# Low part of the third and fourth rows of the first weights, placed ahead of the third rows of Zl in VectorE's order

## The chip, the core and the metric

The kernel runs on one core of a Trainium2 chip. The core has a matrix engine (TensorE, called PE in the profile, with its weight loads as PEld), a vector engine (VectorE, DVE), a scalar engine (ScalarE, ACT), GpSimd (POOL) and a sync engine (SP) that issues most DMAs. Each engine runs its own instructions in the order in which they stand in its program, and waits on semaphores for the others. The metric is the device time of one execution in microseconds (us). A name with "q" behind it (SPq, DVEq) is the engine's sequencer, which issues and waits.

## The reference

One decoder block for x of 512 tokens by 1024 channels: an RMS norm, one wide input projection, two attention branches with 8 heads of 64 each (forgetting attention "f" and block-sparse attention "m"), gates, two projections back, a merge, an output projection and a residual add.

```python
h = rms_norm(x, norm_g[layer])
proj = h @ w_in[layer]
fq, fk, fv, fz, mq, mk, mv, mz, ga, gb, fl = split_cols(proj, IN_SPLITS)
q = rms_norm(to_heads(fq, FOX_HEADS), fox_q_g[layer])
k = rms_norm(to_heads(fk, FOX_HEADS), fox_k_g[layer])
...
merged = (jax.nn.sigmoid(ga + b_gate[layer, 0]) * (y_fox @ w_fox[layer])
          + jax.nn.sigmoid(gb + b_gate[layer, 1]) * (y_moba @ w_moba[layer]))
x = x + merged @ w_out[layer]
```

The change touches only the start: the product of x, scaled by the norm's gain, with the first 256 columns of w_in ("fqa", the queries of the first four forgetting heads).

## The kernel before, in words

**Products in two parts.** Every matrix operand is split into a high part h (rounded by a copy into the type fp32r) and a low part l, which is the operand less its high part. A product is the sum of three: high by high, high by low and low by high. So each operand costs a copy, mostly on ScalarE, and a subtraction on VectorE.

**Rows.** The 1024 channels are eight groups of 128, called rows 0 to 7 here; "the third rows" is row 2 and "the third and fourth rows" are rows 2 and 3. For row k, `XT[k]` is that part of x transposed (128 channels by 512 tokens), loaded as tile xt. `split_x` makes from it Zh (line 130, ScalarE: x times the gain) and Zl (line 132, VectorE). The weights of fqa come in two halves of four rows, loaded as wr_fqa; `first_split` makes wh_fqa (lines 163 or 165) and wl_fqa (line 167). In the first half it takes row 0, row 1 and then rows 2 and 3 together; in the second half rows 4 and 5, then 6 and 7. Its argument `between` says which rows of x are split behind each of these steps.

**First products.** `first_qk` (lines 390 to 392) goes over the eight rows and in each over four groups of 128 tokens: wh by Zh (line 390), wl by Zh (391), wh by Zl (392), 12 matmuls of 256 columns a row. The same function does fka (264 columns) from the same Z. TensorE's order among these three lines within a row is chosen by the planner described below.

**What follows.** The statistics of x give a factor r for each token, which norm_row (line 248) spreads by a transpose into a row rbc (line 249, ScalarE). `normalise` then makes the normalised operand Gh and Gl (lines 253 to 255). The gate products fza and fzb (lines 413 to 415) still use Z; fva (lines 314 to 316) is the first to use Gh and Gl. xf (line 323) is the input of the forget gates, lines 336 to 344 normalise queries and keys (the last steps on GpSimd), line 352 makes the low part of the values fva and so frees their bank of PSUM. Lines 459 to 497 compute the forget gates on VectorE. The attention, the gates and the output projection follow; the last result is added at line 977 and stored at 979.

**The order.** The program is laid out by a planner that simulates the engines' times and lets each engine take what it expects to be ready first. Where the text says `with behind():`, the instruction is tied behind the one that was last put on VectorE, so that the planner cannot take it out of turn. In the first products every cast and subtraction on VectorE is tied in this way, so VectorE's order there is the order of the text: a chain.

The call (line 1048) and the order that results on VectorE before the change: Zl of row 0, the weights of row 1, Zl of row 1, Zl of row 2, wl of rows 2 and 3, Zl of row 3.

```python
first_split(0, ((0,), (1, 2), (3,)))
first_split(1, ((4, 5), (6, 7)))
```

Of the kernel before, what the change touches and what calls it, by code (L numbers as in the profile page):

```python
# [29 lines left out]
def fox_moba_kernel(ctx: ExitStack, tc, xT, x, w_in, w_fl, w_fox, w_moba, w_out, cst, rope, out):  # L30
# [85 lines left out]
    def behind(engine=mybir.EngineType.DVE):  # L116
        return tc.issue_after(last_on(engine))
# [6 lines left out]
    def split_x(*ks):  # L124
        for k in ks:
            Z[k] = [stage["pool"].tile([P, S], F32R, name=f"Z{hl}{k}") for hl in "hl"]
            for c in (slice(0, 256), slice(256, S)) if k == 0 else (slice(0, S),):
                xt = XT[k][:, c]
                zh, zl = (z[:, c] for z in Z[k])
                A.activation(zh, xt, AF.Copy, scale=col(C_NG + k))  # L130
                with behind():
                    V.scalar_tensor_tensor(zl, xt, col(C_NG + k), zh.bitcast(F32), op0=OP.mult, op1=OP.subtract)
# [21 lines left out]
    def first_split(hf, between):  # L154
        raw = RAW[hf]
        hi = sb.tile([P, 4, 264], F32R, name=f"wh_fqa{hf}", tag="wh", bufs=4)
        lo = sb.tile([P, 4, 264], F32R, name=f"wl_fqa{hf}", tag="wl", bufs=4)
        for q, xs in enumerate(between):
            k = slice(2 * q, 2 * q + 2) if hf else slice(max(q, 2 * q - 2), max(q + 1, 2 * q))

            if hf == 0 and q < 2:
                with behind():
                    V.tensor_copy(hi[:, k, :CW], raw[:, k])
            else:
                A.activation(hi[:, k, :CW], raw[:, k], AF.Copy)
            with behind():
                V.tensor_tensor(out=lo[:, k, :CW], in0=raw[:, k], in1=hi[:, k, :CW].bitcast(F32), op=OP.subtract)
            split_x(*xs)
        chunks.setdefault("fqa", []).append((hi, lo))
# [875 lines left out]
        for u in filler(names):  # L1045
            u()

    first_split(0, ((0,), (1, 2), (3,)))
    first_split(1, ((4, 5), (6, 7)))
    nc.sync.dma_start(out=wfl, in_=w_fl)  # L1050
    load_fl("fka", COLS["fka"], 0)
# [184 lines left out]
```

## Time and profile before

| what | us |
|---|---|
| median of three runs | 425.41 (425.33 to 425.57) |
| the profiled execution | 425.42 |
| its span | 423.7 |
| TensorE busy | 417.6 |
| VectorE busy | 327.4 |
| ScalarE busy | 279.6 |
| GpSimd busy | 101.8 |

The profile is of one execution. A row of the timeline gives the start in us from the span's start, the duration, the engine, the line of the kernel, the operation, the tile written and the tiles read, the shapes and how many instructions are merged in the row; a bracket gives the idle time of the engine ahead of it and who ended it. Matmuls overlap: one of 256 columns shows 0.28 us, though the next starts about 0.12 us behind it. The ends of matmuls are modelled, their starts are measured. A row of the view of waits has the waiting engine, tile and line, whom it waited for, the total in us, how often, and the longest.

### The profile page before, as it was taken

The numbers are of one execution on the slowest core, as the hardware profiler recorded it, in microseconds if no ns is written. First come the engines' busy times: TensorE is split into PE (matmuls) and PEld (weight loads), VectorE is DVE, ScalarE is ACT, GpSimd is POOL, SyncE is SP. The second block draws the span as 40 slices with busy tenths as digits, with TensorE's granted clock in tenths as the row PEclk, the third lists the DMA queues.
The fourth block names the chain that finished last, engine by engine and source line by source line (L and its number), as shares of the span: only waits on it lengthen the run. The fifth ranks groups of instructions, "written<-read, shape, count | busy, mean of one in ns | idle before, by whom it ended". The sixth has DMA issues, their size and how long they took to land.

```text
span 423.7 us, 7681 instructions
## 1 busy us (share of the span) xinstructions
PE 417.6 (99%) x2912; PEld 388.2 (92%) x2912; DVE 327.4 (77%) x575; ACT 279.6 (66%) x528; POOL 101.8 (24%) x120
## 2 busy tenths in 40 slices
PE   7999999999999999999999999999999999999996
PEld 6998899999999998899998888899999989988885
DVE  3669978799968778668666779767979698689883
ACT  5877327877877869569757687656656535686450
POOL 1055620223235550015660100340000000022230
PEclk9999999999999999999999999999999999999999
DMA  7972334576253123213032310673141603697484
GB/s 238 389 282 97 95 105 140 154 214 195 79 179 102 28 100 101 84 42 99 28 99 68 108 50 27 227 259 109 27 176 63 236 2 105 216 252 123 99 138 161
DMA packets 24484, 56.10 MB, mean 132 GB/s; under 512 B 2824, under 2 KB 7616, under 8 KB 24448
## 3 DMA queue, kind: packets, MB, share of 16 engines
q1 hardware_dynamic: 13536, 38.11, 27.3%
q0 software_dynamic: 3392, 8.39, 8.7%
q10 hardware_dynamic: 7520, 9.11, 6.6%
q8 instruction: 23, 0.38, 0.4%
q14 instruction: 13, 0.11, 0.1%
HBM read 48.11 MB, written 6.32 MB: 128 GB/s over the span
## 4 chain that ended last, share of the span: by engine, by line
PE 97%; DMA 1%; SPq 0%; DVE 0%; issue 0%; ACT 0%; DVEq 0%
PE pb_GB L769 3%; PE pb_GA L769 3%; PE pb_GA L766 3%; PE pb_GB L766 3%; PE pb_GB L768 3%; PE pb_GA L768 3%; PE po L957 3%; PE po L956 3%; PE po L955 3%; PE pv L627 2%; PE lg L572 2%; PE pv L626 2%; PE lg L571 2%; PE pf L696 2%; PE pf L695 2%; PE pf L697 2%
## 5 line engine op out<-in xcount | busy, mean ns | idle before, releaser
L342 POOL TENSOR_TENSOR ff<-ss,mh 128x8 f32<-128x8 f32 x16 | 29.5, 1845 | 73.7 <-DVE ss L340 52.1
L576 ACT ACTIVATE p<-p,negm 128x128 f32<-128x128 f32 (+1 forms) x64 | 35.8, 560 | 13.3 <-DVE negm L574 12.3
L574 DVE CUSTOM_DVE_ANT_0 p<-lg,mask 128x128 f32<-128x128 f32 (+1 forms) x64 | 30.8, 486 | 14.9 <-PE lg L572 14.6
L904 POOL DMA_DIRECT2D wr_o<-in_w_out_dram x4 | 4.9, 1224 | 95.6 <-ACT wr_o L903 91.9
L142 DVE TENSOR_TENSOR wl_GA<-wr_ga,wh_GA 128x1024 fp32r<-128x1024 f32 x14 | 16.9, 1223 | 5.8 <-ACT wh_GA L140 3.8
L140 ACT ACTIVATE wh_GA<-wr_ga 128x1024 fp32r<-128x1024 f32 x14 | 14.6, 1060 | 10.0 <-PE pb_GA L768 5.1
L140 ACT ACTIVATE wh_GB<-wr_gb 128x1024 fp32r<-128x1024 f32 x14 | 14.6, 1060 | 9.5 <-PE pm L696 3.5
L571 PE MATMUL lg<-KH,QS 128*128 128x128 f32 (+1 forms) x64 | 20.4, 328 | 0.0
L918 DVE TENSOR_TENSOR wl_o<-wr_o,wh_o 128x1024 fp32r<-128x1024 f32 x14 | 17.0, 1222 | 3.8 <-ACT wh_o L917 3.8
L917 ACT ACTIVATE wh_o<-wr_o 128x1024 fp32r<-128x1024 f32 x14 | 14.8, 1061 | 7.2 <-PE pb_GB L768 2.8
L142 DVE TENSOR_TENSOR wl_GB<-wr_gb,wh_GB 128x1024 fp32r<-128x1024 f32 x14 | 16.9, 1222 | 3.5 <-ACT wh_GB L140 3.5
L652 DVE TENSOR_TENSOR ypair<-pv,ysh 64x512 f32<-64x512 f32 x16 | 11.0, 687 | 6.6 <-ACT ysh L651 6.3
L546 DVE SCALAR_TENSOR_TENSOR KL<-p_kT,cs,KH 64x512 fp32r<-64x512 f32 x16 | 12.0, 748 | 3.4 <-ACT KH L543 3.3
L651 ACT ACTIVATE ysh<-pv 64x512 f32<-64x512 f32 x16 | 9.5, 595 | 7.4 <-PE pv L627 4.2
L623 DVE TENSOR_TENSOR ptl<-p_a,pth 128x512 fp32r<-128x512 f32 x16 | 11.0, 685 | 4.2 <-ACT pth L622 4.2
L336 DVE TENSOR_REDUCE ss<-sq 128x8 f32<-128x512 f32 x16 | 10.8, 680 | 4.4 <-ACT sq L335 4.3
L766 PE MATMUL pb_GA<-Gh,wh_GA 128*128 128x256 f32 x48 | 13.6, 283 | 0.0
L769 PE MATMUL pb_GA<-Gh,wl_GA 128*128 128x256 f32 x48 | 13.5, 281 | 0.0
L768 PE MATMUL pb_GA<-Gl,wh_GA 128*128 128x256 f32 x48 | 13.5, 281 | 0.0
L769 PE MATMUL pb_GB<-Gh,wl_GB 128*128 128x256 f32 x48 | 13.5, 281 | 0.0
L768 PE MATMUL pb_GB<-Gl,wh_GB 128*128 128x256 f32 x48 | 13.4, 281 | 0.0
L766 PE MATMUL pb_GB<-Gh,wh_GB 128*128 128x256 f32 x48 | 13.3, 281 | 0.0
(461 smaller groups left out, 1794.8 us busy)
## 6 DMA issues: line engine op xcount, KB each, us to landing
wr_ga<-in_w_in_dram SPq DMA_DIRECT2D x8, 512.0 KB
wr_gb<-in_w_in_dram SPq DMA_DIRECT2D x8, 512.0 KB
wr_o<-in_w_out_dram SPq DMA_DIRECT2D x8, 512.0 KB
xt<-in_xT_dram SPq DMA_DIRECT2D x8, 256.0 KB
x<-in_x_dram SPq DMA_DIRECT2D x8, 256.0 KB
s_dramh<-sum_sh ACTq DMA_DIRECT2D x8, 256.0 KB
s_draml<-sum_sl ACTq DMA_DIRECT2D x8, 256.0 KB
wr_wf<-in_w_fox_dram SPq DMA_DIRECT2D x4, 512.0 KB
```

The lines of the kernel that those rows point to most:

```text
L140: A.activation(hi[:, :, 0:n], src, AF.Copy)
L142: eng.tensor_tensor(out=lo[:, q, 0:n], in0=src[:, q], in1=hi[:, q, 0:n].bitcast(F32), op=OP.subtract)
L342: G.tensor_tensor(out=f2, in0=ss.rearrange("p t h -> p (t h)"), in1=mh, op=OP.pow)
L571: T.matmul(lg[:, :n], qs[:, qt], kh[:, :n], start=True, stop=False)
L574: V.tensor_tensor_reduce(pt, lg[:, :n], mask[:, 512 - n:512], -0.125, 3.0e38, op0=OP.add, op1=OP.min, accum_out=mkn[:, hh, i:i + 1])
L576: A.activation(pt, pt, AF.Exp, bias=mkn[:, hh, i:i + 1], scale=-1.0, accum_out=rs[:, hh, i:i + 1])
L766: T.matmul(o, hi[:, k, cc], lh, start=(n < 3 and c == 0 and k == 0), stop=False, skip_group_check=True)
L768: T.matmul(o, hi[:, k, cc], ll, start=False, stop=False, skip_group_check=True)
L769: T.matmul(o, lo[:, k, cc], lh, start=False, stop=(k == 3), skip_group_check=True)
L917: A.activation(wide(hi), wide(R[key, c]), AF.Copy)
L918: V.tensor_tensor(out=wide(lo), in0=wide(R[key, c]), in1=wide(hi).bitcast(F32), op=OP.subtract)
L955: T.matmul(o, gh, hi[:, c, r, :], start=(new and k == 0), stop=False, skip_group_check=True)
```

## The change

In the first half of the weights, row 2 of x is no longer split in the step of row 1 but in the last step, with row 3, behind the weights' rows 2 and 3. On VectorE the subtraction wl_fqa of rows 2 and 3 (line 167) now stands in front of Zl of row 2 (line 132), and Zl of row 3 follows as before. ScalarE's order stays Zh of row 1, wh of rows 2 and 3, Zh of row 2, Zh of row 3. The planner, fed with this, also chooses other orders on TensorE inside the first products, on VectorE, ScalarE and GpSimd around 30 to 50 us, and for two instructions on TensorE near 289 and 300 us.

```diff
-    first_split(0, ((0,), (1, 2), (3,)))
+    first_split(0, ((0,), (1,), (2, 3)))
     first_split(1, ((4, 5), (6, 7)))
```

## The prediction, as put on record before the changed kernel ran

> **What bounds the kernel now.** I read the page first: the span, the busy shares, the granted clock and the shares of the chain that ended last.
>
> ```profile
> span 423.7 us, 7681 instructions
> PE 417.6 (99%) x2912; PEld 388.2 (92%) x2912; DVE 327.4 (77%) x575; ACT 279.6 (66%) x528; POOL 101.8 (24%) x120
> PEclk9999999999999999999999999999999999999999
> PE 97%; DMA 1%; SPq 0%; DVE 0%; issue 0%; ACT 0%; DVEq 0%
> ```
>
> TensorE (PE) is busy for 99% of the span at full clock and makes up 97% of the chain. So a microsecond counts only if TensorE stands still in it. The view of the waits, for TensorE alone, lists every such place.
>
> ```profile
> PE warm_ps L104 <- DVE fg_pre L479: 1.1, 1, 1.1
> PE fqa L391 <- DVE wl_fqa L167: 0.7, 1, 0.7
> PE fqa L390 <- DVE wh_fqa L163: 0.5, 1, 0.5
> PE fqa L390 <- ACT Zh L130: 0.3, 1, 0.3
> ```
>
> There are four, all in the first products. The change aims at the second: line 391 waits for a low part of the first weights. After it TensorE waits for nobody until its last product. The timeline around it, in order of time (start, duration, engine, line):
>
> ```profile
> 7.75 0.75 DVE L132 SCALAR_TENSOR_TENSOR Zl<-xt,cs,Zh 128x512 fp32r<-128x512 f32 x1
> 7.94 0.63 ACT L165 ACTIVATE wh_fqa<-wr_fqa 128x512 fp32r<-128x512 f32 x1 [0.84 <-DMA wr_fqa<-in_w_in_dram]
> 8.78 1.38 ACT L130 ACTIVATE Zh<-xt,cs 128x512 fp32r<-128x512 f32 x2 [0.21 <-DMA xt<-in_xT_dram]
> 9.54 0.75 DVE L132 SCALAR_TENSOR_TENSOR Zl<-xt,cs,Zh 128x512 fp32r<-128x512 f32 x1 [1.05 <-ACT Zh L130]
> 9.56 0.73 PE L390 MATMUL fqa<-wh_fqa,Zh 128*128 128x256 f32 x4 [0.28 <-ACT Zh L130]
> 10.21 0.68 DVE L167 TENSOR_TENSOR wl_fqa<-wr_fqa,wh_fqa 128x512 fp32r<-128x512 f32 x1
> 10.95 0.39 PE L391 MATMUL fqa<-wl_fqa,Zh 128*128 128x256 f32 x1 [0.66 <-DVE wl_fqa L167]
> 12.00 0.28 PE L390 MATMUL fqa<-wh_fqa,Zh 128*128 128x256 f32 x1
> ```
>
> VectorE (DVE) ends the Zl of the second rows at 8.50 and then idles 1.05 us for the third rows' Zh. The inputs of the low part have been there since 8.57 (7.94 + 0.63), but it stands behind that Zl and runs only at 10.21. TensorE, through with its four line-390 products, waits for it until 10.95.
>
> **The change part by part.** Nothing is added or taken away: the same instructions run with the same operands, no DMA changes its place on SP's, ACT's or POOL's queue, and only VectorE's order is meant to change: low part (L167), then the third rows' Zl, then the fourth rows'.
>
> *Low part.* It can start when ScalarE's high part ends, 8.57, plus the handoff seen at the Zl (Zh's first half of the 1.38 us ends at 8.78 + 0.69 = 9.47, the Zl starts at 9.54: 0.07). So it runs 8.64 to 9.32, inside the 1.05 us in which VectorE idles. Price: nothing.
>
> *The Zl behind it.* Its input comes at 9.47 and VectorE is free at 9.32, so it stays at 9.54 and ends at 10.29. The fourth rows' Zl moves up to 10.21 from 10.81.
>
> *TensorE.* Its undisturbed pace is shown by
>
> ```profile
> 13.44 0.64 PE L390 MATMUL fqa<-wh_fqa,Zh 128*128 128x256 f32 x4
> 13.92 0.64 PE L391 MATMUL fqa<-wl_fqa,Zh 128*128 128x256 f32 x4
> ```
>
> four products in 0.48 us, 0.12 each; four in a group show 0.64. The group at 9.56 shows 0.73, so its restart after a wait cost 0.09, which stays. Line 391 could then begin at 9.56 + 0.09 + 0.48 = 10.13 instead of 10.95: **0.82 us**. The eight products from 10.95 to 12.00 took 1.05 where eight at pace take 0.96; that second restart, **0.09 to 0.10**, goes as well. In the changed program four line-391 products stand ahead of four line-392, so the Zl is needed at 10.13 + 0.48 = 10.61 and is there at 10.29, with 0.32 to spare. Sum at the fourth rows: **0.92 us**. The nearest rows bound it: 0.66, what the row at 10.95 itself counts as idle, and 1.0, if the first restart shrinks too. I take 0.92, since starts are measured while ends of products are modelled.
>
> *What is late next.* The fourth rows start at 11.08; their Zh (second half of the 1.38) is there at 10.16. The fifth start at 12.50, and the later rows at 1.42 each, so the first products end near 18.1 and fka begins there. Its second line needs these:
>
> ```profile
> 14.94 1.06 ACT L140 ACTIVATE wh_fka<-wr_fka 128x1024 fp32r<-128x1024 f32 x1 [0.61 <-DMA wr_fka<-in_w_in_dram]
> 16.04 1.23 DVE L142 TENSOR_TENSOR wl_fka<-wr_fka,wh_fka 128x1024 fp32r<-128x1024 f32 x1 [0.52 <-ACT wh_fka L140]
> 19.56 0.29 PE L391 MATMUL fka<-wl_fka,Zh 128*128 128x264 f32 x1
> ```
>
> The low part of fka ends at 17.27 and is now wanted at 19.56 - 0.92 = 18.64: 1.37 us of cover are left, and a wait would begin only when a DMA of these weights came later than that.
>
> *VectorE from 30 to 60 us.* The program is laid out by a planner, and it also reorders here: two small xf (L323) and one reduction (L336) move ahead of the eight normalising instructions (L253).
>
> ```profile
> 30.38 0.23 DVE L323 SCALAR_TENSOR_TENSOR xf<-fka,r,cs 128x8 f32<-128x8 f32 x1 [0.99 <-ACT qn_fka L321]
> 30.56 0.60 ACT L249 ACTIVATE rbc<-p_rbc 128x512 f32<-128x512 f32 x1 [0.29 <-PE p_rbc L248]
> 31.19 3.31 DVE L253 SCALAR_TENSOR_TENSOR xt<-xt,cs,rbc 128x512 f32<-128x512 f32 x4 [0.58 <-ACT rbc L249]
> 39.26 1.27 DVE L336 TENSOR_REDUCE ss<-sq 128x8 f32<-128x512 f32 x2
> 57.54 0.41 DVE L352 TENSOR_TENSOR v_fva<-pj_fva,v_fva 128x256 fp32r<-128x256 f32 x1
> 59.12 0.28 PE L314 MATMUL pj_fva<-wh_fva,Gh 128*128 128x256 f32 x1
> ```
>
> From 31.19 on VectorE has no idle time until 60. The squares for the moved reduction go in front of rbc on ScalarE, which by the rows puts rbc's end near 31.3 and L253 near 31.4, 0.2 later than now; in return 0.6 for the reduction and some 0.14 for each xf leave the stretch. It ends 0.6 to 0.9 earlier, almost in step with TensorE. Who waits for its end is the third fva product, whose bank L352 frees: 57.95 against 59.12, 1.17 us of cover. If the stretch did not move at all, 0.25 would be left. Price: nothing.
>
> *The rest.* Two more swaps on TensorE, near 289 and 300 us (p_rinv behind one product, one L768 behind some others), change its order and not its work. Later order on VectorE, ScalarE and POOL is unchanged, and every transfer there starts when a buffer is freed, so it moves with TensorE. The end moves whole:
>
> ```profile
> 419.90 0.28 PE L957 MATMUL po<-wh_o,mg 128*128 128x256 f32 x1
> 420.22 0.42 DVE L977 TENSOR_TENSOR ot<-po,eo 128x256 f32<-128x256 f32 x1 [0.88 <-PE po L957]
> 420.67 0.36 SPq L979 DMA_DIRECT2D out_dram<-ot  x1
> ```
>
> Sum: the profiled execution took 425.42, its span 423.70 and 1.72 around it; 425.42 - 0.92 = **424.50 us**. The median of the runs shown, 425.41, is the same within 0.01.
>
> **The rivals.**
>
> *Part of the gain only.* The 0.32 us ahead of the Zl is thin. If the low part starts over 0.2 us later than I have it, it pushes the Zl; with 0.66 gained the time is 424.76, and with the bound of half the gain lost 424.96. For it: handoffs of 0.1 to 0.2 us in the rows. Against it: both inputs are early.
>
> *It does not do what it says.* If the low part were held by something other than its place, it would still end near 10.9: 425.42. The 1.05 us of idle time with its inputs ready speak against it.
>
> *VectorE's stretch slips, and the time ends slower.* POOL's multiplications of fka (L344) move with the reduction from 50.64 to two places inside the stretch. The rows show that such a neighbour costs VectorE time:
>
> ```profile
> 50.64 2.38 POOL L344 TENSOR_TENSOR qn_fka<-qn_fka,ff 128x512 f32<-128x512 f32 x2
> 51.01 1.04 DVE L468 TENSOR_SCALAR fg<-fg 128x32 f32<-128x32 f32 x1
> 52.35 1.75 DVE L142 TENSOR_TENSOR wl_fqb<-wr_fqb,wh_fqb 128x1024 fp32r<-128x1024 f32 x1
> 55.51 1.21 DVE L142 TENSOR_TENSOR wl_fqb<-wr_fqb,wh_fqb 128x1024 fp32r<-128x1024 f32 x1
> 57.44 0.17 DVE L474 SCALAR_TENSOR_TENSOR fg<-fg,fg 128x32 f32<-128x32 f32 x1
> ```
>
> Beside it a small operation took 1.04 instead of some 0.17 and a low part 1.75 instead of 1.21: 1.4 us lost already. Two full holds would be 2.38, so the move is worth between 1.4 less and 1.0 more. The Trainium skill, SBUF — State Buffer, section "Who interferes with whom", says that a VectorE instruction with two SBUF inputs and a GpSimd instruction that reads SBUF exclude each other for the whole instruction; the 1.75 agrees. By that rule alone, with both moved multiplications holding a neighbour fully, the time would be at most 424.65. The place is the third fva product: with the 1.0 the stretch ends 0.4 later at worst than now, TensorE waits 0.15, and 424.65 results. A stretch later by 1.17 than now takes the whole gain (425.42), and later by 2.02 makes the kernel slower by 0.85; at 2.5 the time would be 426.75. That needs 1.6 us more than the rows give, so the chance is small, mostly for planner moves that I have not seen through.
>
> **How the numbers follow.** Forecast (424.35 to 424.65): 0.68. Part of the gain: 0.15. Nothing gained: 0.08. Slower: 0.09. A measurement of this kernel tells about 0.2% from no change, 0.85 us, so faster begins below 424.56; the forecast lies only 0.06 under that line, and I put 0.56 of its 0.68 below it, with 0.02 from the others. Faster 0.58, same 0.33, slower 0.09. The range 424.3 to 425.0 takes in the bounds 0.66 and 1.0 and the half gain, and leaves out nothing gained, slower and about 0.02 under it.
>
> **What would show it.** Right: L167 starts at 8.6 on VectorE, the third rows' Zl stays at 9.54, line 391 loses its wait, the fourth rows start near 11.1, fka near 18.1, and the last product starts near 419.0. Wrong: the low part runs after 9.5, a wait of line 392 on Zl, a wait of the third fva product on L352, or a shift at 18 us that is smaller at 420.

## The result, and the profile after

| | before | changed |
|---|---|---|
| median | 425.41 us (16 runs, 424.94 to 425.97) | 424.62 us (16 runs, 424.15 to 424.99) |
| ratio, 95% interval | | 0.9981 (0.9974 to 0.9989) |
| the profiled execution, its span | 425.42, 423.7 | 424.43, 422.5 |

The changed kernel is 0.79 us faster by its medians; the interval goes from 0.47 to 1.11 us. That is 0.19%, just short of the 0.2% that the prediction took as the line between "same" and "faster". A later comparison of the same two kernels, with 29 and 11 runs, gave 0.77 us by the medians (ratio 0.9985, 0.9976 to 0.9993).

The page of the changed kernel, and TensorE's waits:

```profile
span 422.5 us, 7680 instructions
PE 417.3 (99%) x2912; PEld 388.0 (92%) x2912; DVE 327.5 (78%) x575; ACT 279.7 (66%) x528; POOL 102.4 (24%) x120
PE 97%; DMA 1%; SPq 0%; DVE 0%; issue 0%
```

```profile
PE warm_ps L104 <- DVE fg_pre L479: 1.1, 1, 1.1
PE fqa L390 <- DVE wh_fqa L163: 0.5, 1, 0.5
```

Of the four waits two are gone: line 391 on the low part, which the change was aimed at, and line 390 on the third rows' Zh, which it was not. (The wait of warm_ps that stays is not one of the first products, as the prediction has it: it is that of the warm-up matmuls ahead of them, at 1.11 us.) The timeline of the place, as it was shown of before:

```profile
7.80 0.63 ACT L165 ACTIVATE wh_fqa<-wr_fqa 128x512 fp32r<-128x512 f32 x1 [0.84 <-DMA wr_fqa<-in_w_in_dram]
8.47 0.69 DVE L167 TENSOR_TENSOR wl_fqa<-wr_fqa,wh_fqa 128x512 fp32r<-128x512 f32 x1
8.51 1.39 ACT L130 ACTIVATE Zh<-xt,cs 128x512 fp32r<-128x512 f32 x2
9.27 1.41 DVE L132 SCALAR_TENSOR_TENSOR Zl<-xt,cs,Zh 128x512 fp32r<-128x512 f32 x2
9.29 0.74 PE L390 MATMUL fqa<-wh_fqa,Zh 128*128 128x256 f32 x4
9.87 0.63 PE L391 MATMUL fqa<-wl_fqa,Zh 128*128 128x256 f32 x4
10.34 0.63 PE L392 MATMUL fqa<-wh_fqa,Zl 128*128 128x256 f32 x4
10.82 0.28 PE L390 MATMUL fqa<-wh_fqa,Zh 128*128 128x256 f32 x1
```

The low part (L167) runs from 8.47 to 9.16, before the third rows' Zh is ready; the Zl follows at 9.27, and line 391 starts 0.58 us behind line 390, which is four products at pace and one restart. Here the third rows' Zh also came 0.27 us earlier than in the profile of before (8.51 against 8.78): its transfer landed earlier. So the two profiled spans differ by more than the medians do.

To take that luck out, I read from the timelines where the first product of each row starts on TensorE (its line-390 group). In us:

```
kernel                       2nd rows  3rd rows  4th rows  3rd to 4th  4th to last product
before                         7.52      9.56     12.00      2.44         407.90
before, again                  7.45      9.21     11.64      2.44         407.90
changed                        7.58      9.29     10.82      1.52         407.85
changed, again                 7.66      9.50     11.03      1.52         407.88
row 2 alone ahead              7.50      9.52     11.03      1.52         407.83
both Zl ahead                  7.57      9.21     12.31      3.10         408.26
one dose                       8.17      9.81     11.63      1.82         407.86
two doses                      7.62      9.52     11.83      2.31         407.85
late weights, changed order    8.12      9.73     11.63      1.91         407.88
late weights, old order        7.47      9.09     10.90      1.81         407.88
row by row                     7.97      9.59     11.01      1.42         407.86
row by row, again              7.67      9.09     10.51      1.42         407.88
row by row, old order          7.53      9.13     11.07      1.94         407.82
```

The last two columns are differences taken before rounding. The first two columns wander with the first transfers, by up to 0.7 us between kernels that load in the same order. In the second profile of the changed kernel no transfer sets the second rows' start: TensorE itself is late there, because its products in the first rows start 0.21 us apart instead of 0.12 until about 7.3 us. The column "3rd to 4th" does not wander: 2.44 twice before, 1.52 twice after. That is the change: **0.92 us**. And from the fourth rows to the last product every kernel but one takes 407.82 to 407.90 us, so what is gained at 11 us is still there at the end. The 1.24 us by which the last product came earlier in the first pair of profiles are 0.92 from this column and 0.33 from the landing of the third rows, less 0.06 for the second rows, and 0.05 from the rest.

The end of the changed kernel moved whole:

```profile
418.67 0.28 PE L957 MATMUL po<-wh_o,mg 128*128 128x256 f32 x1
418.98 0.42 DVE L977 TENSOR_TENSOR ot<-po,eo 128x256 f32<-128x256 f32 x1 [0.88 <-PE po L957]
```

### The profile page after: what moved, and what is told of

It reads as the page before. It is cut to its first block, busy times and chain, and to the rows that moved or that the text cites. A ratio compares the mean times of both kernels' runs of the same rounds, so it can differ in the third digit from the quotient of the medians.

```text
span 422.5 us, 7680 instructions
## 1 busy us (share of the span) xinstructions
PE 417.3 (99%) x2912; PEld 388.0 (92%) x2912; DVE 327.5 (78%) x575; ACT 279.7 (66%) x528; POOL 102.4 (24%) x120
## 4 chain that ended last, share of the span: by engine, by line
PE 97%; DMA 1%; SPq 0%; DVE 0%; issue 0%
PE pb_GB L769 3%; PE pb_GA L769 3%; PE pb_GA L766 3%; PE pb_GB L766 3%; PE pb_GB L768 3%; PE pb_GA L768 3%; PE po L957 3%; PE po L956 3%; PE po L955 3%; PE pv L627 2%; PE lg L572 2%; PE pv L626 2%; PE lg L571 2%; PE pf L696 2%; PE pm L697 2%; PE pf L697 2%
## 5 line engine op out<-in xcount | busy, mean ns | idle before, releaser
L142 DVE TENSOR_TENSOR wl_GA<-wr_ga,wh_GA 128x1024 fp32r<-128x1024 f32 x14 | 16.9, 1222 | 5.9 <-ACT wh_GA L140 3.9
L142 DVE TENSOR_TENSOR wl_GB<-wr_gb,wh_GB 128x1024 fp32r<-128x1024 f32 x14 | 16.9, 1221 | 3.5 <-ACT wh_GB L140 3.5
```

The costliest lines, as they stand in the source:

```text
L142: eng.tensor_tensor(out=lo[:, q, 0:n], in0=src[:, q], in1=hi[:, q, 0:n].bitcast(F32), op=OP.subtract)
```

## The experiments

Two theories besides mine were open after the result. Mine is A (place): the gain is the wait that went with the low part's place. B (layout): the planner's other order further on is part of it. C (landing): part of it is chance of the first transfers. The rival that each expectation names is the one for that run.

### Before again

No edit.

> The kernel before once more, unchanged, for a second profile of it and its spread. Theory A (place): line 391 waits again 0.6 to 0.9 us for the low part of rows 2 and 3, whenever the third rows' Zh comes, since the low part always starts one Zl (0.67 us) behind that Zh; the time is 425.4 within 0.3. Theory C (landing): the start of the third rows' Zh, 8.78 us in the first profile of before and 8.51 in that of the changed kernel, is chance of the first transfers and lies between 8.4 and 9.0 here too; if C is wrong and the change itself made it earlier, it is at 8.7 to 8.8 again.

Measured: 425.27 us (ratio 1.0002, 0.9993 to 1.0011). TensorE's wait and the rows around it:

```profile
PE fqa L391 <- DVE wl_fqa L167: 0.7, 1, 0.7
```

```profile
8.43 1.37 ACT L130 ACTIVATE Zh<-xt,cs 128x512 fp32r<-128x512 f32 x2
9.19 0.75 DVE L132 SCALAR_TENSOR_TENSOR Zl<-xt,cs,Zh 128x512 fp32r<-128x512 f32 x1 [0.77 <-ACT Zh L130]
9.21 0.74 PE L390 MATMUL fqa<-wh_fqa,Zh 128*128 128x256 f32 x4
9.85 0.68 DVE L167 TENSOR_TENSOR wl_fqa<-wr_fqa,wh_fqa 128x512 fp32r<-128x512 f32 x1
10.59 0.39 PE L391 MATMUL fqa<-wl_fqa,Zh 128*128 128x256 f32 x1 [0.65 <-DVE wl_fqa L167]
```

The unchanged kernel has the third rows' Zh at 8.43 here, 0.35 earlier than in its first profile, and no wait on Zh. So that wait comes and goes with the landing, and C is right for it. The wait of line 391 is the same 0.65: the low part follows the Zl, and the Zl follows the Zh, wherever that falls.

### Row 2's low part alone ahead

```diff
-            with behind():
-                V.tensor_tensor(out=lo[:, k, :CW], in0=raw[:, k], in1=hi[:, k, :CW].bitcast(F32), op=OP.subtract)
+            for kk in ((slice(2, 3), slice(3, 4)) if hf == 0 and q == 2 else (k,)):
+                with behind():
+                    V.tensor_tensor(out=lo[:, kk, :CW], in0=raw[:, kk], in1=hi[:, kk, :CW].bitcast(F32), op=OP.subtract)
+                if kk == slice(2, 3):
+                    split_x(2)
...
-    first_split(0, ((0,), (1,), (2, 3)))
+    first_split(0, ((0,), (1,), (3,)))
```

> The changed kernel with its low part cut in two: row 2's in front of the third rows' Zl, row 3's behind it (two instructions of some 0.43 us in place of one of 0.68). Theory A: only row 2's low part ends the wait of line 391, so the whole gain stays: no wait of line 391, the same 424.6 within 0.3, fourth rows' first product within 0.1 us of one row's pace behind the third rows'. Rival: if row 3's low part must be ahead too, TensorE waits some 0.3 us in the fourth rows and the time is 424.9.

Measured: 424.56 us (0.9984, 0.9975 to 0.9993); third to fourth rows 1.52, as with both rows ahead. Only row 2's low part was late; row 3's has time behind the Zl.

TensorE's own order inside the third rows changed too: before, lines 391 and 392 take turns, and in the changed kernel each line's four products stand together. The gain does not hang on that. Here lines 390 and 391 take turns in the third rows and the stretch is the same 1.52; the two doses below keep the groups of four and need 2.31.

### Both Zl ahead

```diff
-    first_split(0, ((0,), (1,), (2, 3)))
+    first_split(0, ((0,), (1, 2, 3), ()))
```

> The opposite of the change: the third and the fourth rows' Zl both stand ahead of the low part of rows 2 and 3. Theory A: the low part moves behind a second Zl, so the wait of line 391 grows by one Zl, 0.67 us, to some 1.3, and the time is 0.67 above before (426.1), 1.5 above the changed kernel. Theory B (the planner's other order further on is part of the gain): the planner lays out the program behind 20 us anew here, and the lag of TensorE's products against before changes by over 0.3 us between 20 and 420 us; by A it stays within 0.15.

Measured: 426.40 us (1.0032, 1.0019 to 1.0046).

```profile
9.19 1.42 DVE L132 SCALAR_TENSOR_TENSOR Zl<-xt,cs,Zh 128x512 fp32r<-128x512 f32 x2 [0.64 <-ACT Zh L130]
10.52 1.29 DVE L167 TENSOR_TENSOR wl_fqa<-wr_fqa,wh_fqa 128x512 fp32r<-128x512 f32 x2
11.26 0.38 PE L391 MATMUL fqa<-wl_fqa,Zh 128*128 128x256 f32 x1 [1.32 <-DVE wl_fqa L167]
```

The wait is 1.32 in place of 0.65, one Zl (0.67) more, and third to fourth rows 3.10, 0.67 above before. That is A's number. The time, though, is 1.06 above the 425.34 of before that it was compared with, not 0.67: the table's last column is 408.26 here, 0.36 more than before. So B holds for this kernel: its program is laid out anew behind 20 us, and in its one profile that layout costs 0.36. A good part lies at one place, where TensorE transposes p_ri and the next product starts 0.31 us later. At all seven such transposes of before, and at the other six here, it starts 0.03 us later:

```profile
254.69 0.27 PE L596 MATMUL p_ri<-ident,rinv 128*8 128x128 f32 x1
255.00 0.51 PE L695 MATMUL pf<-yhf,wh_wf 128*128 128x512 f32 x1
```

For the change itself B is worth little: its last column differs from that of before by 0.05 and 0.02.

### One and two doses in front of the low part

```diff
+            for i in range(1 if hf == 0 and q == 2 else 0):
+                with behind():
+                    V.tensor_tensor(out=rbc, in0=mask, in1=mask, op=OP.add)
             with behind():
                 V.tensor_tensor(out=lo[:, k, :CW], in0=raw[:, k], in1=hi[:, k, :CW].bitcast(F32), op=OP.subtract)
```

The second kernel has range(2). What the extra instruction writes into rbc is overwritten later by line 249's copy.

> The changed kernel with one extra VectorE instruction of some 0.68 us (its result is overwritten later and not used) in front of the low part. It starts at 8.5 where VectorE is free, so the low part ends 0.5 us later and the third rows' Zl 0.2 to 0.5 later than in the changed kernel. Theory A with its cover of 0.32 us ahead of line 392: a loss of 0 where the third rows' Zh starts at 8.78, and of 0.3 (0.2 of wait and 0.1 of restart) where it starts at 8.5: 424.6 to 424.9. If there were no cover, the loss would be the whole 0.68 and the time 425.3.

> The changed kernel with two extra VectorE instructions of some 0.68 us (results not used) in front of the low part. With one dose 0.3 us was lost. Theory A (the low part's end and then the third rows' Zl set TensorE's start, with a small cover): the second dose is past all cover and is lost whole, so line 391 waits some 0.5 to 0.7 us and line 392 is late too: 425.5 to 425.7, about the time of before. Rival (VectorE's order has no price of its own here, the loss with one dose was chance of the first transfers): 424.6 to 425.0 again.

Measured: one dose 424.93 us (0.9988, 0.9980 to 0.9997), third to fourth rows 1.82, 0.30 more than the changed kernel; two doses 425.57 us (1.0002, 0.9993 to 1.0011), 2.31, 0.79 more. Two doses of the kind:

```profile
8.52 1.41 DVE L170 TENSOR_TENSOR rbc<-mask 128x512 f32<-128x512 f32 x2
9.52 0.74 PE L394 MATMUL fqa<-wh_fqa,Zh 128*128 128x256 f32 x4
9.85 0.68 DVE L172 TENSOR_TENSOR wl_fqa<-wr_fqa,wh_fqa 128x512 fp32r<-128x512 f32 x1
10.45 1.41 DVE L132 SCALAR_TENSOR_TENSOR Zl<-xt,cs,Zh 128x512 fp32r<-128x512 f32 x2
10.59 0.74 PE L395 MATMUL fqa<-wl_fqa,Zh 128*128 128x256 f32 x4 [0.33 <-DVE wl_fqa L172]
11.25 0.74 PE L396 MATMUL fqa<-wh_fqa,Zl 128*128 128x256 f32 x4
```

The low part ends at 10.53 and line 391 (here L395) starts 0.06 later; the Zl is late too, so the line-392 group (L396) starts 0.66 behind it instead of 0.48, with a second restart. The loss grows as a chain with a cover would have it: 0.30 with one dose, 0.79 with two. The second dose cost 0.49, not its whole 0.68 as expected. By the table two doses give back 0.79 of the 0.92; by the medians (425.57 against 425.49 before) all of it.

### Late weights, with the new and the old order

Both kernels load the third rows of x ahead of the weights' rows 2 and 3; the first has the changed order on VectorE, the second that of before.

```diff
-        AFTER = {0: ((0, 1),), 1: ((1, 2), (2, 4)), 3: ((4, 6),), 5: ((6, 8),)}
+        AFTER = {0: ((0, 1),), 1: ((1, 2),), 2: ((2, 4),), 3: ((4, 6),), 5: ((6, 8),)}
```

> The changed order on VectorE, but the third rows of x are loaded ahead of the weights' rows 2 and 3, so that Zh of row 2 comes ahead of the high part (on ScalarE too). Theory A: the low part in front then holds a Zl whose input is there; line 391 waits as long as in the sister kernel with the old order, line 392 waits a second time, 0.2 us, and the change turns into a loss: 0.2 to 0.3 us slower at the fourth rows than the sister kernel. Rival (the low part ahead is better in any case, since line 391 comes ahead of 392): no wait of line 392, 0.2 us or more faster than the sister.

> The sister: the old order on VectorE with the same order of loads (third rows of x ahead of the weights' rows 2 and 3). Theory A: the Zl fits into the time in which VectorE waits for the high part, so the wait of line 391 shrinks from 0.8 to some 0.4 us, and the time is 424.8 to 425.0 without the change. Rival: the wait stays at 0.8 and the time at 425.3.

Measured: changed order 424.98 us (0.9982, 0.9965 to 0.9998) and 1.91 from third to fourth rows; old order 424.75 us (0.9979, 0.9969 to 0.9989) and 1.81. The rows of the changed order:

```profile
8.32 0.72 ACT L130 ACTIVATE Zh<-xt,cs 128x512 fp32r<-128x512 f32 x1 [0.45 <-DMA xt<-in_xT_dram]
8.98 0.63 ACT L165 ACTIVATE wh_fqa<-wr_fqa 128x512 fp32r<-128x512 f32 x1
9.64 0.69 DVE L167 TENSOR_TENSOR wl_fqa<-wr_fqa,wh_fqa 128x512 fp32r<-128x512 f32 x1 [0.55 <-ACT wh_fqa L165]
10.25 1.41 DVE L132 SCALAR_TENSOR_TENSOR Zl<-xt,cs,Zh 128x512 fp32r<-128x512 f32 x2
10.39 0.74 PE L391 MATMUL fqa<-wl_fqa,Zh 128*128 128x256 f32 x4
11.05 0.74 PE L392 MATMUL fqa<-wh_fqa,Zl 128*128 128x256 f32 x4
```

Now the low part in front waits 0.55 us for its own input, while the Zl behind it could run: Zh was ready at 9.04 (8.32 + 0.72). Line 392 starts 0.66 behind line 391 instead of 0.48. With the old order line 391 still waits, but some 0.24 us, less than the 0.4 that was expected: it starts at 9.85, where its pace behind line 390 would put it at 9.61. The same edit that gained 0.92 loses 0.1 at the fourth rows here, in one profile of each, with the sign that A gave and less than its 0.2 to 0.3. The medians (424.98 and 424.75) agree in sign, but their intervals overlap. So the loss is shown by the rows and not by the times; that the gain is gone is shown by both. What the change is worth depends on which of the two inputs comes first.

### Row by row

```diff
-        AFTER = {0: ((0, 1),), 1: ((1, 2), (2, 4)), 3: ((4, 6),), 5: ((6, 8),)}
+        AFTER = {0: ((0, 1),), 1: ((1, 2), (2, 3)), 2: ((3, 4),), 3: ((4, 6),), 5: ((6, 8),)}
...
-            k = slice(2 * q, 2 * q + 2) if hf else slice(max(q, 2 * q - 2), max(q + 1, 2 * q))
+            k = slice(2 * q, 2 * q + 2) if hf else slice(q, q + 1)
...
-    first_split(0, ((0,), (1,), (2, 3)))
+    first_split(0, ((0,), (1,), (2,), (3,)))
```

A third kernel has the same loads and parts with the old order: `first_split(0, ((0,), (1, 2), (), (3,)))`.

> The changed kernel, with the weights' rows 2 and 3 loaded, rounded and subtracted one by one: row 2's weights, third rows of x, row 3's weights, and on VectorE each row's low part in front of its Zl. Theory A: what is left at the third rows is the landing of x; with 128 KB less ahead of it, it comes some 0.3 us earlier, line 390 no longer waits there, and the time is 424.2 to 424.5, 0.1 to 0.4 below the changed kernel. Rival (the transfers' rate is not what sets that landing, or the smaller pieces cost as much): 424.6 or above.

> The changed kernel once more, for a second profile and beside the two others. Measured from the second rows' first product to the fourth rows' first, before took 4.48 and 4.19 us in its two profiles and the changed kernel 3.24. Theory A: 3.2 to 3.6 again (more than 3.24 only by what the third rows' Zh comes late), no wait of line 391, and the time 424.5 to 424.7. Rival (the 1.24 us by which the first profile of the changed kernel was ahead belong to the change): the last product again 1.1 to 1.3 us ahead of the first profile of before and a time near 424.2.

> The row-by-row kernel once more, beside the changed kernel on the same chip. Theory A: the stretch from the second to the fourth rows is 3.0 to 3.1 again, at TensorE's pace, whatever the landings, and the time is 0.2 to 0.4 below the changed kernel. Rival: its 424.28 was a lucky set of runs, and it is within 0.1 of the changed kernel.

> The row-by-row loads and parts, but with the third rows' Zl ahead of row 2's low part, the order of before. Theory A: only the order is undone, and what the order is worth returns, now with a low part of one row: line 391 waits 0.4 us and restarts at 0.1, the stretch is 3.5, the time 0.5 above the row-by-row kernel (424.8). Rival (row by row, the order no longer matters because the smaller pieces come early): the time of the row-by-row kernel within 0.1.

Measured: row by row 424.28 us (0.9968, 0.9955 to 0.9980), and in a second set, beside the two others, 424.29 (0.9984, 0.9974 to 0.9994); changed again 424.54 (0.9985, 0.9976 to 0.9993); row by row in the old order 424.50 (0.9986, 0.9978 to 0.9995).

```profile
8.20 0.42 DVE L167 TENSOR_TENSOR wl_fqa<-wr_fqa,wh_fqa 128x256 fp32r<-128x256 f32 x1
8.62 0.75 DVE L132 SCALAR_TENSOR_TENSOR Zl<-xt,cs,Zh 128x512 fp32r<-128x512 f32 x1
9.09 0.64 PE L390 MATMUL fqa<-wh_fqa,Zh 128*128 128x256 f32 x4
9.57 0.63 PE L391 MATMUL fqa<-wl_fqa,Zh 128*128 128x256 f32 x4
10.04 0.63 PE L392 MATMUL fqa<-wh_fqa,Zl 128*128 128x256 f32 x4
10.51 0.64 PE L390 MATMUL fqa<-wh_fqa,Zh 128*128 128x256 f32 x4
```

Here TensorE goes through the third rows without a restart: 1.42 from third to fourth rows, 12 products at 0.12. The median is 0.25 to 0.34 below that of the changed kernel, the lowest of all. The times do not settle the lead: beside each other on one chip the two kernels have ratios of 0.9984 and 0.9985, and three of the twelve row-by-row runs took 425.4 to 426.0. The table shows it, 0.10 from third to fourth rows and more from second to fourth: 3.03 and 2.84 against 3.24 and 3.36. The second of these missed the expected 3.0 to 3.1, since in that profile the second rows had no restart either. The expected earlier landing of the third rows is seen in one of the two profiles only: their Zh starts at 8.54 and 7.86, against 8.51 and 8.72 in the changed kernel. Loads and parts were changed together, so which of them removes the wait is not shown. Undoing only the order costs 0.52 in the table (1.94 against 1.42), the expected 0.5; the medians differ by 0.21 (424.50 against 424.29), and the ratios, 0.9986 and 0.9984, by less still. The rival of the changed kernel's second run, that its 1.24 was its own, fell: its last product started 0.99 ahead of the first profile of before.

## Why the prediction was right, point by point

**The low part at no price, at 8.64.** Right: 8.47 and 8.48 in the two profiles of the changed kernel, in VectorE's gap, 0.04 behind the high part. The handoff of 0.07 was read too large: the prediction halved the merged row of two Zh, 1.38, but a single Zh takes 0.72, and the Zl follows it by 0.04 or less.

**0.82 us of wait and 0.10 of restart.** Right: the two profiles of each kernel give 2.44 less 1.52, twice 0.92.

**A cover of 0.32 us ahead of line 392.** Right. In the changed kernel the third rows' Zl starts at 9.27 and, with the 0.75 of a single Zl, ends at 10.02; line 392 starts at 10.34. In its second profile these are 10.23 and 10.55, again 0.32. With one dose the Zl is 0.48 later against line 390: 0.32 of it is cover, 0.16 is left, and with a restart of 0.1 that is most of the 0.30 that was lost. The rival "part of the gain only" asked for a low part over 0.2 us later than worked out; it was earlier.

**VectorE from 30 to 60 us.** The sign was right, the size too small. The stretch's end, as line 352 shows it, came 1.60 earlier, not 0.6 to 0.9:

```profile
30.98 2.98 DVE L253 SCALAR_TENSOR_TENSOR xt<-xt,cs,rbc 128x512 f32<-128x512 f32 x4
48.14 1.80 POOL L344 TENSOR_TENSOR qn_fka<-qn_fka,ff 128x512 f32<-128x512 f32 x1
48.94 1.04 DVE L468 TENSOR_SCALAR fg<-fg 128x32 f32<-128x32 f32 x1
51.35 1.15 DVE L142 TENSOR_TENSOR wl_fqb<-wr_fqb,wh_fqb 128x1024 fp32r<-128x1024 f32 x1
55.94 0.41 DVE L352 TENSOR_TENSOR v_fva<-pj_fva,v_fva 128x256 fp32r<-128x256 f32 x1
57.96 0.28 PE L314 MATMUL pj_fva<-wh_fva,Gh 128*128 128x256 f32 x1
```

Part of the 1.60 is the early landing in this pair, since TensorE's own product at this place came 1.16 earlier. The length of the stretch, from line 253 to line 352, is free of that: it fell by 1.39 (26.35 to 24.96), and by 1.40 between the second profiles (26.52 to 25.12). The prediction's terms, the reduction and two xf, make some 0.88 of it. The bank is free at 56.35 and wanted at 57.96: the cover grew from 1.17 to 1.61, and from 1.00 to 1.44 between the second profiles.

What the sum missed is the low part of fqb (L142), which fell from 1.75 to 1.15, and from 1.67 to 1.16 in the second profiles. The slower rival stood on GpSimd's moved multiplications, and beside one L468 again took 1.04 and ended within 0.04 of it. Alone it takes 0.17, as the second profile of before shows, where it ran just ahead of them. The sentence of the Trainium skill that the prediction cites (SBUF — State Buffer, "Who interferes with whom") speaks of two SBUF inputs; L468 reads one tile, so its hold is a measurement of these runs. Three other kernels show when the low part is held: before again, both Zl ahead and two doses, in this order.

```profile
50.62 0.17 DVE L468 TENSOR_SCALAR fg<-fg 128x32 f32<-128x32 f32 x1
50.96 3.02 POOL L344 TENSOR_TENSOR qn_fka<-qn_fka,ff 128x512 f32<-128x512 f32 x2
51.41 1.67 DVE L142 TENSOR_TENSOR wl_fqb<-wr_fqb,wh_fqb 128x1024 fp32r<-128x1024 f32 x1 [0.23 <-ACT wh_fqb L140]
```

```profile
52.67 1.27 POOL L344 TENSOR_TENSOR qn_fka<-qn_fka,ff 128x512 f32<-128x512 f32 x1
53.30 1.73 DVE L142 TENSOR_TENSOR wl_fqb<-wr_fqb,wh_fqb 128x1024 fp32r<-128x1024 f32 x1
```

```profile
49.19 2.95 POOL L348 TENSOR_TENSOR qn_fka<-qn_fka,ff 128x512 f32<-128x512 f32 x2
52.95 1.16 DVE L142 TENSOR_TENSOR wl_fqb<-wr_fqb,wh_fqb 128x1024 fp32r<-128x1024 f32 x1
```

With both Zl ahead the two multiplications stand apart (the first ends at 51.00, the second starts at 52.67), and the low part is still held, because it starts beside the second. With two doses they follow each other, and the low part is free, because it starts after both. So what counts is whether the low part meets a multiplication, not how the multiplications stand to each other; in the changed kernel the planner's new places happened to keep them apart.

**The rest neutral.** Right for this change (0.05 and 0.02). It is no rule: in the kernel with both Zl ahead the planner's new layout cost 0.36.

**The sum.** 424.50 was forecast, with 424.3 to 425.0 as the range; measured 424.62. By the timelines the change is worth 0.92, by two comparisons of medians 0.79 and 0.77, with intervals that include 0.92. Whether the 0.13 to 0.15 between them is real stays open: a profile shows one execution, and none that was taken shows a landing at which the gain is smaller. The likelier side of the bet missed by a hair: 0.58 stood on a time below 424.56, 0.33 on "same", and 424.62 is 0.06 above the line.

**What I had wrong beside it.** The sum has no term for the spread of the runs; the three that were shown lay within 0.24 us. The 16 runs of before span 1.03 us, and kernels that load in the same order start the second rows anywhere from 7.45 to 8.17. The list of waits was also taken for complete. It is not: in the second profile of before the third rows' group at 9.21 shows 0.74, a restart, with no wait listed.

## What to carry to other kernels

Where an engine works through a fixed order, compare for each neighbour when its input is there: an instruction whose inputs are early belongs ahead of one that waits, and the same swap loses as soon as the inputs come the other way round (0.92 gained, 0.1 lost here). Behind a wait on the engine that bounds the kernel, count the restart too. To read a gain below a microsecond from a profile, measure between two events of the same engine that lie behind the last chance landing, not from the span.

## What the runs showed of the hardware that was not expected

- From the second rows on, after a wait, TensorE's second product starts 0.19 to 0.23 us behind the first instead of 0.12; a group of four then shows up to 0.74 instead of 0.64. It also showed in groups with no listed wait (9.29 in the changed kernel), where the idle time was hidden behind the modelled end of the product ahead.
- In the first rows products start 0.21 us apart for a while, until about 5.8 us in the first profile of before and about 7.3 us in the second of the changed kernel, although the granted clock reads 1.00 in both.
- The same loads in the same order put the start of the second rows anywhere from 7.45 to 8.17 us in the profiles here, a spread of 0.72 against the 0.92 of the whole change.
- Beside a GpSimd multiplication a small VectorE instruction that reads one tile (L468) took 1.04 us; without it, 0.17.
